# Block sums made in place, residual additions moved forward, and a second small buffer for the attention's features

## The chip, the cores and the metric

The kernel runs on one core of a Trainium2 chip. The metric is the device time of one execution in microseconds. The core has a matrix engine (TensorE, PE in the rows; PEld is its weight load), VectorE (DVE), ScalarE (ACT), GpSimd (POOL) and SyncE (SP), which here only issues DMA transfers. Each engine works through its own queue in order; a wait at the head of a queue holds everything behind it.

## The reference

Two transformer blocks in float32 over 1024 tokens of width 1024. The change touches the end of the first block (windowed attention, its residual and norm) and all of the second:

```python
def rmsnorm(x, g):
    xf = x.astype(jnp.float32)
    y = xf * lax.rsqrt(jnp.mean(xf * xf, axis=-1, keepdims=True) + EPS)
    return (y * g.astype(jnp.float32)).astype(x.dtype)

def short_conv_mixer(h, w_in, conv_w, w_out, on_grid):
    gate_b, gate_c, hv = jnp.split(h @ w_in, 3, axis=-1)
    u = gate_c * hv
    conv = conv3_grid(u, conv_w) if on_grid else conv3_seq(u, conv_w)
    return (gate_b * conv) @ w_out

def swiglu(h, w_in, w_out):
    gate, up = jnp.split(h @ w_in, 2, axis=-1)
    return (jax.nn.silu(gate) * up) @ w_out

# second block
x = x + g1 * short_conv_mixer(modulate(rmsnorm(x, norm1_g[i]), sh1, sc1), ...)
x = x + g2 * swiglu(modulate(rmsnorm(x, norm2_g[i]), sh2, sc2), ...)
return rmsnorm(x, final_g)
```

## The kernel before

Every float32 product is made of three matmuls of a rounded high part and a remainder: a cast on ScalarE (L106) and a subtraction on VectorE (L107) split an operand. The large products of the second block use a scheme of seven block products P1 to P7 in place of eight. It needs sums of blocks: of the activations B11, B12, B21, B22 the sums T1 to T4, of the weights the sums S1 to S4.

The stages, by the trace: mixer A of the first block to some 1010 us; projections and attention to 1620; then in the second block N1, the normed activations' sums and the first weight products (`right_operands`, `eight`, to 1712); the conv mixer's sets (`run_sets`, to 1882), which end with `spill`: a finished group of blocks goes to DRAM and GpSimd makes T1 to T4 from it; the conv mixer's output (`out_products` with `conv_use`, to 1980), where products come in the order P1, P2, P6, P7, P5, P4, P3, each with a use of its four tiles of 128 tokens; N3, the second norm and the first FFN products (to 2067, `third`, `right_operands`, `eight`); the FFN's sets (`run_sets` with `gated_up`, to 2476); its output (`out_products` with `ffn_use`, to 2708).

What sets the order: the program is written in plain order, and the tile scheduler sets each engine's queue by a timeline of its own. Work that runs beside the products is cut into steps, which `mix.tick()` hands out. Buffers come from rings, and a buffer's next writer waits for its last reader. Four things of that kind matter here.

- RAW: a ring of four buffers of 1024 columns (`next_raw`), through which weights to be split, normed tiles (xn), features (hs) and reloaded halves (h1) pass, one after another in the order of the calls.
- Units: 18 pieces of SBUF of 512 columns, `U(i)`, E in the rows. `run_sets` and `spill` take them from a list and put them back; the list is first in, first out. In the FFN's sets a gate's activation (L1706) writes to such a unit, and so do the copies out of PSUM (L1283, L1302).
- pages and raws: in `out_products` an operand comes by DMA into a raw buffer, and its split goes to a page. The conv mixer's output has eight pages and four raws.
- xsr: two buffers of a whole tile, into which `conv_use` and `ffn_use` load the residual x in P4 and P3.

In the attention's tail `keep_half` transposes half a tile (L941), evacuates it into the one buffer of `hs2` on ScalarE (L946) and VectorE (L948) and stores it; `last` squares a tile into `junk`, only to have the sum.

Of the kernel before, what the change touches and what calls it, by code (L numbers as in the profile page):

```python
# [10 lines left out]
ALU = mybir.AluOpType  # L11
# [5 lines left out]
NFF = 22  # L17
# [10 lines left out]
def program(tc, I, out):  # L28
# [4 lines left out]
    with ctx:  # L33
# [145 lines left out]
        mix = Mix()  # L179
# [626 lines left out]
        hs2 = ring([ZX[:, 1024:1536]])  # L806
# [7 lines left out]
        junk = sb(P2, "junk", 512)  # L814
# [357 lines left out]
        def right_operands(where, t, h1, h2, eng):  # L1172
# [104 lines left out]
        def run_sets(sets, where, units):  # L1277
# [12 lines left out]
            for n, (st, use) in enumerate(sets):  # L1290
# [72 lines left out]
        def spill(dst, j, even, odd, units):  # L1363

            (b11, b12), (b21, b22) = even, odd
            ids = [units.get() for _ in range(4)]
            t1, t2, t3, t4 = (U(i) for i in ids)
            if b11 is None:
                ids += [units.get() for _ in range(2)]
                b11, b21 = (U(i) for i in ids[4:])  # L1370
                SY.dma_start(b11, dst["B11"][j])
                SY.dma_start(b21, dst["B21"][j])
            else:
                SY.dma_start(dst["B11"][j], b11)
                SY.dma_start(dst["B21"][j], b21)
# [3 lines left out]
            G.tensor_tensor(t2, b12, t1, ALU.subtract)  # L1379
            SY.dma_start(dst["T2"][j], t2)  # L1380
            G.tensor_tensor(t3, b12, b22, ALU.subtract)
            SY.dma_start(dst["T3"][j], t3)
            G.tensor_tensor(t4, b11, t2, ALU.subtract)
            SY.dma_start(dst["T4"][j], t4)
            units.put(*ids)

        def sums_steps(w, j, dst, a, b):

            def block(m, k):
                return w[(2 * j + k - 1) * 128:(2 * j + k) * 128, (m - 1) * 512:m * 512]  # L1390

            def s0():
                SY.dma_start(a, block(2, 2))
                SY.dma_start(b, block(2, 1))

            def s1():
                G.tensor_tensor(a, a, b, ALU.add)
# [414 lines left out]
```

## Time and profile before

| | |
|---|---|
| median of three runs | 2709.69 us (2708.47 to 2711.11) |
| the profiled execution | 2709.77 us, its span 2708.0 us |
| mean granted clock of TensorE | 0.981 |
| PE busy | 2588.4 us (96%), 13666 matmuls |
| DVE busy | 1841.7 us (68%) |
| ACT busy | 1102.5 us (41%) |
| POOL busy | 656.7 us (24%) |

The span is the time from the first to the last instruction of one execution; 1.8 us lie around it. Busy is the time in which an engine had an instruction in work. PE is idle for 119.6 us; the granted clock is the share of full speed that the chip allowed the matrix engine. What an idle stretch ended with is inferred from the semaphores: the engine and line named are the last that came.

### The profile page before, as it was taken

What the parts mean: (1) busy time and instruction counts of PE and PEld (TensorE: products, weight loads), DVE (VectorE), ACT (ScalarE), POOL (GpSimd) and SP (SyncE); (2) the same over time, 40 slices, a digit from 0 to 9 for tenths busy, and PEclk for the clock granted to TensorE, in tenths of its full rate; (3) what the DMA queues carried; (4) which work ended last, traced back from release to release, by engine and by line L of the source; (5) the groups of instructions that cost most, each with busy time, mean ns of one, the idle gap of its engine ahead of it and who ended that gap; (6) DMA issues with size and microseconds to landing.
All of it is one profiled execution on the core that took longest, in us unless ns stands there. A gap on an engine that the chain in (4) does not pass through costs nothing. (4 is left out here: it accounts for less than half of the span.)

```text
span 2708.0 us, 37147 instructions
## 1 busy us (share of the span) xinstructions
PE 2588.4 (96%) x13666; PEld 2216.0 (82%) x13666; DVE 1841.7 (68%) x3013; ACT 1102.5 (41%) x1979; POOL 656.7 (24%) x634
## 2 busy tenths in 40 slices
PE   8999999999999999999999987999878999999998
PEld 5799998879999778888888876877756877787876
DVE  5677775666778875456677977678566765667536
ACT  4332334322233435345556875223454232334433
POOL 2110000010002412313345762041321345302111
PEclk9999999999999999999999998999989999999999
DMA  7454333364444435541364325356554478538643
GB/s 258 141 148 122 101 119 125 121 205 135 130 137 133 146 103 189 174 155 61 92 244 133 98 78 167 109 183 194 179 181 149 151 253 260 181 103 287 195 151 129
DMA packets 344938, 421.18 MB, mean 156 GB/s; under 512 B 18918, under 2 KB 207870, under 8 KB 344242
## 3 DMA queue, kind: packets, MB, share of 16 engines
q1 hardware_dynamic: 337012, 407.80, 47.0%
q10 hardware_dynamic: 7744, 11.01, 1.1%
q8 instruction: 107, 1.75, 0.3%
q14 instruction: 75, 0.61, 0.1%
HBM read 324.84 MB, written 93.91 MB: 155 GB/s over the span
## 5 line engine op out<-in xcount | busy, mean ns | idle before, releaser
L106 ACT CAST w<-raw 128x1024 fp32r<-128x1024 f32 (+1 forms) x234 | 221.7, 958 | 437.5 <-DMA raw<-in_a_w_in 121.9
L107 DVE TENSOR_TENSOR w<-raw,w 128x1024 fp32r<-128x1024 f32 (+1 forms) x232 | 288.1, 1253 | 152.7 <-ACT w L106 148.3
L1265 PE MATMUL PS<-H,w 128*128 128x512 f32 x1404 | 336.8, 395 | 14.1 <-ACT E L1302 10.7
L1265 PEld LDWEIGHTS PS<-H,w 128*128 128x128 f32 x1404 | 267.2, 191 | 74.5 <-ACT E L1302 12.3
L516 PE MATMUL PS<-H,w 128*128 128x320 f32 x2112 | 320.5, 309 | 1.0 <-DVE TT L525 1.0
L516 PEld LDWEIGHTS PS<-H,w 128*128 128x128 f32 x2112 | 310.8, 188 | 3.1 <-DVE TT L525 1.3
L1456 PE MATMUL PS<-H 128*128 128x512 f32 x924 | 220.4, 397 | 12.3 <-ACT H L106 10.5
L1456 PEld LDWEIGHTS PS<-H 128*128 128x128 f32 x924 | 176.7, 192 | 52.3 <-ACT H L106 12.2
L339 POOL TENSOR_TENSOR H<-ACC,H 128x256 fp32r<-128x256 f32 x52 | 50.3, 968 | 609.6 <-ACT H L338 505.1
L320 DVE SCALAR_TENSOR_TENSOR ACC<-raw,CO,ACC 128x512 f32<-128x512 f32 x182 | 133.8, 747 | 20.6 <-DMA raw<-in_ada_w 17.9
L516 PE MATMUL PS<-H 128*128 128x320 f32 x960 | 144.7, 309 | 0.0
L516 PEld LDWEIGHTS PS<-H 128*128 128x128 f32 x960 | 141.1, 188 | 0.5
L603 PE MATMUL PS<-w,H 128*128 128x512 f32 x600 | 140.1, 391 | 0.0
L1265 PE MATMUL PS<-HB,w 128*128 128x512 f32 x540 | 135.7, 400 | 2.9 <-ACT E L1302 2.5
L603 PEld LDWEIGHTS PS<-w,H 128*128 128x128 f32 x600 | 111.5, 188 | 23.3
L107 DVE TENSOR_TENSOR PTR<-PS,PTR 128x512 fp32r<-128x512 f32 x176 | 106.1, 613 | 35.9 <-ACT PTR L106 34.4
L1265 PEld LDWEIGHTS PS<-HB,w 128*128 128x128 f32 x540 | 102.3, 190 | 28.2 <-ACT E L1302 3.4
L1339 PE MATMUL PS<-H,w 128*128 128x512 f32 x408 | 106.2, 413 | 19.3 <-ACT E L1347 9.1
L392 PE MATMUL PS<-H 128*128 128x512 f32 x510 | 120.9, 391 | 0.0
L870 ACT ACTIVATE s<-s,sm 128x641 f32<-128x641 f32 (+1 forms) x128 | 103.3, 808 | 42.6 <-DVE sm L868 42.0
L107 DVE TENSOR_TENSOR H<-raw,H 128x1024 fp32r<-128x1024 f32 x68 | 88.6, 1306 | 46.6 <-ACT H L106 45.2
L106 ACT CAST H<-raw 128x1024 fp32r<-128x1024 f32 x68 | 70.6, 1043 | 110.1 <-DMA raw<-in_a_w_in 63.2
(356 smaller groups left out, 5201.8 us busy)
## 6 DMA issues: line engine op xcount, KB each, us to landing
raw<-in_a_w_in SPq DMA_DIRECT2D x96, 512.0 KB
raw<-in_ada_w SPq DMA_DIRECT2D x80, 512.0 KB
raw<-in_ffn_w_in SPq DMA_DIRECT2D x76, 256.0 KB
E<-in_ffn_w_out SPq DMA_DIRECT2D x66, 256.0 KB
raw<-in_a_w_out SPq DMA_DIRECT2D x32, 512.0 KB
TFT<-E SPq DMA_DIRECT2D x44, 256.0 KB
SFS<-E SPq DMA_DIRECT2D x44, 256.0 KB
raw<-in_b_w_in SPq DMA_DIRECT2D x20, 512.0 KB
```

The costliest lines, as they stand in the source:

```text
L106: A.copy(hi, src)
L107: turn["split"] = (eng or V).tensor_tensor(lo, src, hif, ALU.subtract)
L320: V.scalar_tensor_tensor(ACC[:, s, :], r[:, j, :], CO[:, c, k:k + 1], ACC[:, s, :], ALU.mult, ALU.add)
L339: G.tensor_tensor(AL.r[:, 256:512], ACC[:, s, c], AL.f[:, 0:256], ALU.subtract)
L392: T.matmul(ps, HT[0][:, k, ap, t * 128:(t + 1) * 128], w[:, k % 2, :], start=k == 0 and n == 0, stop=k == 7 and n == 2)
L516: T.matmul(pss[h][:, 0:320], w[:, k, :], HT[0][:, k, ap, h * 320:(h + 1) * 320], start=k == 0 and n == 0, stop=k == 7 and n == 2)
L603: turn["mm"] = T.matmul(accs[t], ys[j].r[:, ap * 640 + t * 128:ap * 640 + (t + 1) * 128], wv[:, j, :], start=kp == 0 and j == 0 and n == 0 ...
L870: A.activation(out=p[:, :nk + 1], in_=p[:, :nk + 1], func=AF.Exp, scale=-1.0, bias=sm[:, j:j + 1], accum_out=sm[:, 2 + j:3 + j])
L1265: turn["mm"] = T.matmul(ps, w[:, k, :], b[:, ap, k, :], start=start and k == 0 and n == 0, stop=k == 3 and n == 2, skip_group_check=not start)
L1339: turn["mm"] = T.matmul(ps, x[:, k, :], b[:, ap, k, :], start=start and k == 0 and n == 0, stop=stop and k == 3 and n == 2, skip_group_che ...
L1456: turn["mm"] = T.matmul(ps[:, t], x[ap][:, i, t * 128:(t + 1) * 128], s[v][:, i, :], start=new and j + i == 0 and q == 0, stop=j + i == nj ...
```

## The change

- `keep_half`: the ring `hs2` has two buffers; the second is `junk`, into which `last` writes its squares.
- `right_operands`: all four subtractions on VectorE; two were on GpSimd for three of four tiles, in N1 and in N3.
- `spill`: T1 overwrites B21, T3 B22, T2 B12, T4 B11, in that order. It takes no units, but T1, T2 and T4 may only be written when the stores of B21, B12 and B11 have landed. `late_spill` is the form with reloaded B11 and B21.
- `sums`: the steps of two pairs are joined, and the ticks over which they are spread doubled; `run_sets` has one `mix.tick()` more.
- The two outputs share `out_use`. x comes by halves: the first half of tiles 0 to 3 is added in P2 and the second half of tiles 4 to 7 in P5 (`gated_add`: GpSimd multiplies and adds, ScalarE squares; x comes through RAW, and the squares go into the same buffer); the other halves come into units, loaded in P7 and P4. xsr is gone. Normed tiles are made by halves, and a conv tile in P3 takes a RAW buffer more (`tmp`).
- The conv mixer's output has seven pages and six raws.

```diff
@@ attention @@
-        hs2 = ring([ZX[:, 1024:1536]])
+        junk = sb(P2, "junk", 512)
+        hs2 = ring([ZX[:, 1024:1536], junk])
@@ right_operands @@
-            eng.tensor_tensor(b22, b12, b22, ALU.subtract)
+            V.tensor_tensor(b22, b12, b22, ALU.subtract)
             V.tensor_tensor(b12, b12, b21, ALU.subtract)
-            eng.tensor_tensor(b11, b11, b12, ALU.subtract)
+            V.tensor_tensor(b11, b11, b12, ALU.subtract)
@@ run_sets @@
                     head(nxt)
+                mix.tick()
@@ spill @@
-        def spill(dst, j, even, odd, units):
+        def spill(dst, j, even, odd):
             (b11, b12), (b21, b22) = even, odd
-            ids = [units.get() for _ in range(4)]
-            t1, t2, t3, t4 = (U(i) for i in ids)
...
-            G.tensor_tensor(t1, b22, b21, ALU.subtract)
-            SY.dma_start(dst["T1"][j], t1)
...
-            units.put(*ids)
+            for name, x in (("B11", b11), ("B21", b21), ("B12", b12)):
+                SY.dma_start(dst[name][j], x)
+            pair_sums(dst, j, b11, b12, b21, b22)
+        def pair_sums(dst, j, b11, b12, b21, b22):
+            for name, o, x, y in (("T1", b21, b22, b21), ("T3", b22, b12, b22), ("T2", b12, b12, b21),
+                                  ("T4", b11, b11, b12)):
+                G.tensor_tensor(o, x, y, ALU.subtract)
+                SY.dma_start(dst[name][j], o)
@@ sums, in the conv's and the FFN's sets @@
-                    mix.begin(sums(c_out, 4, SC, [units.get() for _ in range(4)]), 5)
+                    mix.begin(sums(c_out, 4, SC, [units.get() for _ in range(4)]), 12)
...
-                    mix.begin(sums(f_out, NFF // 2, SF, [units.get() for _ in range(4)]), NFF - 9)
+                    mix.begin(sums(f_out, NFF // 2, SF, [units.get() for _ in range(4)]), 2 * (NFF - 9))
@@ the outputs @@
+        def out_use(X, name, t, ps, done):
+            u2, u3, r, x = U(t), U(4 + t), U(8 + t), U(12 + t)
+            def gated_add(u, gb, i, h):
+                G.tensor_tensor(u, u, gb, ALU.mult)
+                y = next_raw()[:, 0:512]
+                SY.dma_start(y, X[i][:, h * 512:(h + 1) * 512])
+                G.tensor_tensor(u, u, y, ALU.add)
+                mean_square(MS[:, i, h:h + 1], u, y)
+            if name in ("P1", "P6"):
+                A.copy(u2, ps)
+            elif name == "P2":
+                V.tensor_tensor(r, ps, u2, ALU.add)
+                gated_add(r, gbs[0], t, 0)
+            elif name == "P7":
+                SY.dma_start(x, X[t][:, 512:1024])
+            elif name == "P5":
+                A.copy(u3, ps)
+                V.tensor_tensor(u3, PS[:, 4 + t], u3, ALU.add)
+                gated_add(u3, gbs[1], 4 + t, 1)
+            elif name == "P4":
+                V.tensor_tensor(u2, ps, u2, ALU.add)
+                V.tensor_tensor(u2, u2, gbs[1], ALU.mult)
+                V.tensor_tensor(u2, u2, x, ALU.add)
+                SY.dma_start(x, X[4 + t][:, 0:512])
+                mean_square(MS[:, t, 1:2], u2, PS[:, 4 + t])
+                done(t, r, u2)
+            else:
+                tmp = next_raw()[:, 0:512]
+                V.tensor_tensor(tmp, ps, gbs[0], ALU.mult)
+                V.tensor_tensor(x, x, tmp, ALU.add)
+                mean_square(MS[:, 4 + t, 0:1], x, tmp)
+                done(4 + t, x, u3)
...
-        out_products(c_out, 4, TC, SC, pages[2:], [p.f[:, q * 1024:(q + 1) * 1024] for p in pages[:2] for q in range(2)],
+        out_products(c_out, 4, TC, SC, pages[3:], [p.f[:, q * 1024:(q + 1) * 1024] for p in pages[:3] for q in range(2)],
```

Line numbers shift by a few: L1302 keeps its number, the gate's L1706 becomes L1705, the transposes' L1484 L1479, N1's and N3's products L1339 L1340, the output's matmuls L1456 L1451; the multiplication and the addition of `gated_add` are L1608 and L1611.

ScalarE in the FFN's sets, before, from the last copy of one set to the first casts of the next, around the first gate after a `spill`. In brackets stands what a row waits for: DMAHW is a DMA, Pool GpSimd.

```order
L1302 COPY E_13956<-PS_176 128x512 [waits PE_49]
L1706 ACTIVATE E_13956<-E_13956 128x512 [waits DMAHW1_49,DVE_49,Pool_49]
L1302 COPY E_13956<-PS_176 128x512 [waits DMAHW0_49,PE_49]
L106 CAST w2_179<-raw2_183 128x512 [waits DMAHW2_49,PE_49]
L1706 ACTIVATE E_13956<-PS_176 128x512 [waits PE_49]
L106 CAST PA_13953<-raw2_183 128x512 [waits PE_49]
L106 CAST w3_180<-raw3_13954 128x1024 [waits DMAHW7_49,DVE_49,Activation_49]
```

The same place after:

```order
L1302 COPY E_13956<-PS_176 128x512 [waits PE_49]
L1283 COPY E_13956<-PS_176 128x512 [waits PE_49]
L1705 ACTIVATE E_13956<-E_13956 128x512 [waits DVE_49]
L106 CAST w3_180<-raw1_182 128x512 [waits DMAHW5_49,PE_49]
L1705 ACTIVATE E_13956<-PS_176 128x512 [waits PE_49]
L106 CAST PA_13953<-raw1_182 128x512 [waits DMAHW3_49,PE_49]
L1302 COPY E_13956<-PS_176 128x512 [waits DMAHW4_49,PE_49,Pool_49]
L106 CAST w0_177<-raw0_181 128x1024 [waits DMAHW2_49,DVE_49,Activation_49]
```

The gate's activation on a unit (L1706, now L1705) no longer waits for a DMA and GpSimd, and the DMA and GpSimd wait has gone to a later copy, L1302.

GpSimd at P5 in the conv mixer's output, before (L1638 and L1642 are the multiplications of P2 and P5, L1652 the additions of P4, L927 a power for the norm):

```order
L1652 TENSOR_TENSOR E_13956<-E_13956 128x512
L1638 TENSOR_TENSOR E_13956<-E_13956 128x512
L1642 TENSOR_TENSOR E_13956<-E_13956 128x512 x4
L927 TENSOR_TENSOR RM_13958<-RM_13958,mhalf_188 128x1 x2
L1652 TENSOR_TENSOR E_13956<-E_13956 128x512 x2
L927 TENSOR_TENSOR RM_13958<-RM_13958,mhalf_188 128x1 x2
```

And after:

```order
L1608 TENSOR_TENSOR E_13956<-E_13956 128x512 x2
L1611 TENSOR_TENSOR E_13956<-E_13956,raw3_13954 128x512
L1608 TENSOR_TENSOR E_13956<-E_13956 128x512
L1611 TENSOR_TENSOR E_13956<-E_13956,raw1_182 128x512
L1608 TENSOR_TENSOR E_13956<-E_13956 128x512
L1611 TENSOR_TENSOR E_13956<-E_13956,raw0_181 128x512
L1611 TENSOR_TENSOR E_13956<-E_13956,raw1_182 128x512
L927 TENSOR_TENSOR RM_13958<-RM_13958,mhalf_188 128x1 x8
```

The additions of P5 now stand between its multiplications, each on a RAW buffer. On SyncE the buffer raw3 then takes a load of `ffn_w_in`, and after that the last load of `conv_w_out` for P4, with the loads of x for tiles 6 and 7 between; before, the loads of `conv_w_out` stood ahead of P5.

## Rows read from the trace of the kernel before

**Rows 1.** What PE waits for, whole span: engine, releaser, us in total, times, longest.

```profile
PE PS L1484 <- ACT raw L1489: 13.2, 6, 4.1
PE PS L1265 <- ACT E L1302: 13.2, 6, 4.9
...
PE PS L1339 <- ACT w L106: 7.7, 4, 4.5
...
PE PS L998 <- ACT ZX L946: 4.1, 3, 2.3
...
PE PS L1265 <- ACT E L1283: 2.0, 1, 2.0
```

**Rows 2.** Timeline of PE in the FFN's sets: start, us, work, [idle before <- releaser].

```profile
2215.72 7.36 PE L1265 MATMUL PS<-H,w 128*128 128x512 f32 x24 [2.41 <-ACT E L1302]
...
2247.78 2.96 PE L1265 MATMUL PS<-HB,w 128*128 128x512 f32 x12
...
2259.26 7.38 PE L1265 MATMUL PS<-H,w 128*128 128x512 f32 x24 [2.99 <-ACT E L1302]
...
2306.09 6.20 PE L1265 MATMUL PS<-H,w 128*128 128x512 f32 x14 [4.93 <-ACT E L1302]
```

**Rows 3.** Timeline of ScalarE at the same places.

```profile
2214.56 0.63 ACT L1706 ACTIVATE E<-E 128x512 f32<-128x512 f32 x1 [13.69 <-DMA TFT<-E]
...
2258.10 0.63 ACT L1706 ACTIVATE E<-E 128x512 f32<-128x512 f32 x1 [14.74 <-DMA TFT<-E]
...
2304.93 0.63 ACT L1706 ACTIVATE E<-E 128x512 f32<-128x512 f32 x1 [16.21 <-DMA TFT<-E]
```

**Rows 4.** Timeline of SyncE's DMA issues: B21 and T4 of one pair.

```profile
2200.74 0.37 SPq L1375 DMA_DIRECT2D TFB<-E  x1
...
2209.92 0.38 SPq L1384 DMA_DIRECT2D TFT<-E  x1
```

**Rows 5.** Stretches: busy us of PE, PEld, DVE, ACT, POOL; clock, DMA share, GB/s.

```profile
1920.00:1925.00 5.00, 4.71 (x11) 3.79 (x12) 4.71 (x3) 2.32 (x3) 4.86 (x3) 0.50 0.63 204
...
1995.00:2000.00 5.00, 1.17 (x5) 0.77 (x5) 4.07 (x11) 3.47 (x8) 0.55 (x1) 0.50 0.82 271
...
2305.00:2310.00 5.00, 3.91 (x9) 3.14 (x10) 4.07 (x6) 2.56 (x5) 2.31 (x2) 0.52 0.56 197
```

**Rows 6.** Timeline in the conv's P6: PE, SyncE, ScalarE.

```profile
1920.29 11.93 PE L1456 MATMUL PS<-H 128*128 128x512 f32 x39 [6.32 <-ACT H L106]
...
1909.10 7.38 SPq L121 DMA_DIRECT2D H<-SCS  x2
...
1919.19 1.04 ACT L106 CAST H<-H 128x1024 fp32r<-128x1024 f32 x1 [2.94 <-DMA H<-SCS]
```

**Rows 7.** Groups in 1950 to 2030: shapes, count | busy us, mean ns | idle before.

```profile
L922 ACT ACTIVATE E<-E 128x512 f32<-128x512 f32 x16 | 10.1, 629 | 17.8 <-DVE E L1655 8.0 <-DVE E L1664 7.5 <-DVE RM L926 1.3
...
L1652 POOL TENSOR_TENSOR E<-E 128x512 f32<-128x512 f32 x2 | 2.6, 1291 | 4.0 <-DMA E<-X 4.0
...
L107 DVE TENSOR_TENSOR w<-raw,w 128x1024 fp32r<-128x1024 f32 x1 | 1.2, 1226 | 3.8 <-ACT w L106 3.8
```

**Rows 8.** Timeline, P5 to N3: ScalarE, GpSimd, VectorE, PE.

```profile
1952.35 0.58 ACT L1640 COPY E<-PS 128x512 f32<-128x512 f32 x1
...
1954.57 7.02 POOL L1642 TENSOR_TENSOR E<-E 128x512 f32<-128x512 f32 x4 [29.71 <-DVE E L1641]
...
1963.07 0.69 DVE L1653 TENSOR_TENSOR E<-PS,E 128x512 f32<-128x512 f32 x1 [2.63 <-PE PS L1456]
...
1999.95 3.35 PE L1339 MATMUL PS<-H,w 128*128 128x512 f32 x7 [0.54 <-ACT H L1167]
```

**Rows 9.** Timeline of VectorE and GpSimd side by side.

```profile
2442.60 1.67 DVE L1245 TENSOR_TENSOR raw<-raw 128x512 f32<-128x512 f32 x1
...
2442.04 1.68 POOL L1377 TENSOR_TENSOR E<-E 128x512 f32<-128x512 f32 x1 [1.23 <-DVE E L1708]
```

**Rows 10.** Timeline of ScalarE in N1.

```profile
1663.35 1.14 ACT L1167 CAST HB<-E 128x512 fp32r<-128x512 f32 x2 [2.69 <-POOL E L1179]
```

More of the change, by code (lines that the diff above doesn't have):

```diff
@@ L1421, in sums @@
             steps = []
             for j in range(0, nj, 2):
-                two = [sums_steps(w, i, dst, U(bufs[2 * (i - j)]), U(bufs[2 * (i - j) + 1])) for i in range(j, min(j + 2, nj))]
-                for x in zip(*two) if len(two) == 2 else [(y,) for y in two[0]]:
-                    steps.extend(x)
+                two = [pair(j + i, U(bufs[2 * i]), U(bufs[2 * i + 1])) for i in range(min(2, nj - j))]
+                steps.extend(lambda x=x: [y() for y in x] for x in zip(*two))
             return steps
@@ L1549, in program @@
             halves[n]["late"](N1, (2 * n, 2 * n + 1), late_uses[n])
-        units = Units(14, 15, 8, 9, 10, 11, 12, 13)
-        spill(TC, 0, (None, U(16)), (None, U(17)), units)
-        units.put(16, 17)
+        late_spill(TC, 0, U(16), U(17), U(14), U(15))
+        units = Units(8, 9, 10, 11, 12, 13, 14, 15, 16, 17)
         c_sets = []
@@ L1578, in use @@
                 free()
-                spill(TC, j, *((cv[:, 0:512], cv[:, 512:1024]) for cv in cvs), units)
+                spill(TC, j, *((cv[:, 0:512], cv[:, 512:1024]) for cv in cvs))
                 cvs.clear()
                 if j == 1:
-                    mix.begin(sums(c_out, 4, SC, [units.get() for _ in range(4)]), 5)
+                    mix.begin(sums(c_out, 4, SC, [units.get() for _ in range(4)]), 12)
                 mix.tick()
@@ L1672, in program @@
+            if name == "P3" and t < 3:
+                if t:
+                    halves[t + 1]["load"]()
+                halves[t + 1]["early"](N3, ((0, 6), (1, 7), (2, 0))[t], early_up(t + 1))
         pages = slot_pages((4, 2, 3, 5, 1))
-        out_products(c_out, 4, TC, SC, pages[2:], [p.f[:, q * 1024:(q + 1) * 1024] for p in pages[:2] for q in range(2)],
+        out_products(c_out, 4, TC, SC, pages[3:], [p.f[:, q * 1024:(q + 1) * 1024] for p in pages[:3] for q in range(2)],
                      conv_use)
@@ L1695, in program @@
             if f % 2:
-                spill(TF, f // 2, (None, U(ys[0])), (None, U(ys[1])), units)
-                units.put(*ys)
+                b11, b21 = units.get(), units.get()
+                late_spill(TF, f // 2, U(ys[0]), U(ys[1]), U(b11), U(b21))
+                units.put(*ys, b11, b21)
                 ys.clear()
@@ L1711, in use @@
                 if f % 2:
-                    spill(TF, f // 2, *((U(a), U(b)) for a, b in ys), units)
+                    spill(TF, f // 2, *((U(a), U(b)) for a, b in ys))
                     units.put(*ys[0], *ys[1])
@@ L1729, in program, with fourth @@
             SY.dma_start(gbs[m], GT[4][m, :].partition_broadcast(128))
-        xsr = ring([U(12, 2), U(14, 2)])
-        def fourth(i, halves):
+        def fourth(i, *xs):
             rms(RX[:, i:i + 1], MS[:, i, :])
```

151 lines of the change are left out of this document (41 added, 110 removed).

## The prediction, as recorded before the run

> **What bounds the kernel now.** TensorE. The reader starts with the busy times: PE works 2588.4 of the span's 2708.0 us, so 119.6 us are idle and an edit can win only from those, from the low clock that follows a stop, or lose by adding to them. The second view is the table of PE's waits [rows 1]: the largest groups lie in the parts that the change rewrites. The third is the timeline around the stops.
>
> In the FFN's sets PE stops at 2215.72, 2259.26 and 2306.09, each time for a copy of ScalarE (L1302) [rows 2]. ScalarE has the gate's activation L1706 queued ahead of it, and that one waits 13.7, 14.7 and 16.2 us for a store of T sums [rows 3]: its output goes to a unit that `spill` took for T4, and T4's store, issued at 2209.92, lets ScalarE go only at 2214.56, 13.8 us after the pair's B21 went out at 2200.74 [rows 3, 4]. In the conv mixer's output PE stops 6.3 us at 1920.29: SyncE held two loads for 7.4 us because the four raw buffers were not free, and the cast came 2.9 us after the last of them [rows 6]. At the change from conv to FFN the transposes wait 13.2 us in all for the evacuations [rows 1].
>
> After a stop the granted clock is low: 0.52 in the 5 us around the end of the stop of 4.9 us, 0.50 after that of 6.3 us [rows 5]; 0.50 is the lower of its two levels, 1.2 GHz. So a stop is paid twice. Twelve matmuls take 2.96 us, 0.24 each; the 24 after the first two stops took 7.36 and 7.38 instead of 5.8, the 14 after the third 6.20 instead of 3.4 [rows 2].
>
> **The change part by part.** Times are against the profiled run, 2709.77 us (span and 1.8 around it), 0.1 us above the median.
>
> *In-place T sums.* `spill` takes no units any more, T1 to T4 overwrite the pair. In the new order the gate's activation after a pair waits for VectorE alone (the order of ScalarE above); the next writer of a unit that a T store still reads comes 146 matmuls or more, some 35 us, after the pair is complete, where before it came after some 14. T1 now waits for B21's store, which adds a landing of 2 to 5 us to a chain of four subtractions and their stores that took 13.8 us; 35 minus 19 leaves 16 us. So three stops go: 2.41 + 2.99 + 4.93 = 10.3 us, and with them 1.6 + 1.6 + 2.8 = 6.0 us of slow matmuls. The loads of the next weights stand behind T1 and T3 on SyncE, but stood behind T1, T2 and a sum before. The least is nothing, if a weight load becomes late instead; the most 16. I take -15. In the conv's sets one stop of 2.0 us, for a copy into a unit (L1283 [rows 1]), goes for the same reason: -2 (0 to -2.5).
>
> *Six raws and seven pages.* The two loads that were held 7.4 us find buffers; the stop of 6.3 us goes and so do 3 us at half clock (4.7 us of matmuls at 0.50 [rows 5] and a remainder). Four T's of the last pair come one store later, before their first reader still. -8.5 (-5 to -9.5).
>
> *Right operands on VectorE.* Six subtractions in N1 go to VectorE, some 0.69 us each like L1653 [rows 8], 4 us in all. ScalarE's weight casts, for which PE waited 7.7 us in all there and in N3, 4.5 at once [rows 1], stood at 1664.40 right behind casts that waited 2.7 us for a subtraction of GpSimd [rows 10]; now they stand ahead of them. Of the wait and some 1.2 us at a low clock behind it I count most, less what VectorE's longer queue takes back: -4 (-6 to 0).
>
> *Attention.* The second buffer for hs takes away the wait for the store of the features between a tile's halves; the thrown-away squares now wait for that store instead, and later products start a little later. PE's waits for the features' evacuation, 4.1 us [rows 1], are the most that can go, and I count 3 of them lost again: -1 (-4 to +3).
>
> *Additions moved into P2, P5 and P7.* This part costs. In P5, tile t's second half is multiplied and added on GpSimd, squared on ScalarE, and the x it adds sits in a RAW buffer. The RAW ring has four buffers, and the load of `ffn_w_in` behind it and the two loads of `conv_w_out` for P4 take the same buffers in turn. Count from T0, the end of P5's tile 0, which the first L1640 copy dates at 1952.35 [rows 8]. GpSimd's first multiplication begins 2.2 us later [rows 8], its order is mult, mult, add, mult, add, mult, add, add, each 1.29 us alone [rows 7] or 1.76 as the four L1642 took [rows 8]. The third ends at 6.1 to 7.5; the square (0.63 [rows 7], and some 0.2 to read its sum) frees raw3 at 7 to 8.3; a load with its issue takes some 2.9 (the distance in [rows 6]); cast 1.04 [rows 6] and subtraction 1.23 [rows 7] free raw3 again at 12 to 13.5; the second load lands at 15 to 16.5. The cast that feeds P4 also stands behind the square of tile 3, whose x could be loaded only after tile 1's square: 2.2 + 5 operations + 0.8 + 2.9 + one more addition + 0.8 is 14.5 to 17.3. With the cast P4 starts at 16 to 18.5. PE has 24 matmuls until then, 5.8 us: a new stop of 10 to 13 us, where none is now, with 2.4 us of half clock behind it. I take a start at 17.5, near the upper end, because VectorE does two-input work there. Before, P4's tile 0 was done at T0 + 10.7 (L1653 at 1963.07 [rows 8]); after, 17.5 + 30 matmuls of 0.24 + 2.4 = 27. From there to the first N3 product it took 36.9 us before (1999.95 [rows 8]) with x loads late between; after, the rest of P4 and P3 (60 matmuls, 14.3 us) and then eight groups of transposes in a row, whose evacuations, splits and additions on VectorE I put at 15 to 20 us: 29 to 34, say 32. Sum: 27 + 32 against 47.6, so +11. The best is -2 (no stop), the worst +16.
>
> *N3's second half.* Six RAW takes a tile instead of five, but no late x: +1 (-2 to +5). *FFN output*: the same additions lie behind long products, the P5 to P4 turn used the ring that way already: 0 (-2 to +2). `fourth` is the same work.
>
> Sum: -15 - 2 - 8.5 - 4 - 1 + 11 + 1 = -18.5. **2709.8 - 18.5 = 2691 us.**
>
> One row on the sharing of two engines: beside GpSimd's subtraction of 1.68 us at 2442.04 VectorE's L1245, with two inputs in SBUF, took 1.67 us [rows 9], where an instruction of that size without such company takes 0.69 [rows 8]. The Trainium skill, "SBUF — State Buffer", section "Who interferes with whom", says that a VectorE instruction with two SBUF inputs and a GpSimd instruction that reads SBUF lock each other out for a whole instruction, whichever began first. By that rule GpSimd's eight operations in P5 lie near 1.76 and the total is 2692; by uncontended 1.29 throughout it is 2689. The row agrees with the rule.
>
> **The rivals.**
> *The RAW ring's stop does not come.* The loads could be ordered kindly by chance, or GpSimd could start earlier. For: the row order is only an order. Against: each link is a buffer reuse. Then +11 is -2: 2678.
> *The FFN's stops stay.* ScalarE no longer waits for T4, but the T stores landed late because so much was in flight; the weight casts that stand right behind L1302 could be the next to wait. Against: PE's stops there now all end at L1302. Then -15 is 0: 2706, no change.
> *Slower: N3 stays at the lower clock.* Before, PE ran at 0.50 in 1995 to 2000 [rows 5], among the waiting transposes, until N3's products ran dense. After, tile by tile, a chain through tmp, xn, hs and h1 could be longer than a tile's products; four tiles of 48 matmuls and their transposes are some 14 us each, 56 in all (an estimate from 0.24 a matmul), and at half clock over half of them the loss is 28 us: 2719. It decides if a tile's chain takes over some 18 us. Against: I add up 13.6 us for it, the tile's additions, square, evacuations and splits at the prices of [rows 7, 8].
> *The change doesn't do what it says* for units: the list of units could hand a T unit back at once, and the FFN's and the conv's stops would stay: -17 is 0, 2708. The order above speaks against it.
>
> **How the numbers follow.** The forecast has 0.62, its own range is 2683 to 2699. No ring stop 0.15, FFN stops stay, for either reason, 0.14, low clock in N3 0.06, something unnamed 0.03. The range 2677 to 2707 takes the first three in. A measurement tells some 0.2%, 5.4 us, from no change. Faster: 0.62 + 0.15 + 0.04 of the third = 0.81. Same: 0.11. Slower: 0.08.
>
> **What would show it.** In the trace after: no wait of ScalarE's gate for a T store in the FFN's sets, and PE's waits for L1302 down from 13.2 to about 3; no 6.3 us stop in the conv's P6; a stop of some 10 to 13 us right before P4's first matmul, ended by the cast of a `conv_w_out` load; about 59 us from P5's tile 0 to N3's first product. Wrong would be: the FFN part of the span not shorter by over 10 us, or the stretch of the conv's end not longer.

## The result and the profile after

The changed kernel takes 2735.4 us (median of four runs, 2733.3 to 2736.1) against 2710.4 us of the kernel before beside it: a ratio of 1.0092, 95% interval 1.0074 to 1.0109. It is 25 us slower, where 2691 us was forecast with 2707 us as the upper end. The profiled execution took 2735.2 us, its span 2733.4 us, at a mean granted clock of 0.977 (0.981 before).

What PE waits for in the changed kernel, whole span (engine, releaser, us in total, times, longest), beside [rows 1]:

```profile
PE PS L1451 <- ACT H L106: 20.9, 5, 11.0
PE PS L1265 <- ACT E L1302: 11.7, 4, 5.1
...
PE PS L1479 <- ACT raw L1484: 9.2, 3, 4.0
PE PS L941 <- DVE ZX L934: 7.2, 3, 5.6
PE PS L1340 <- ACT w L106: 6.5, 4, 2.5
...
PE PS L1479 <- DVE raw L1647: 3.1, 2, 2.2
```

Three things are to be seen. The waits for L1302, 13.2 us before, are still 11.7: most of the gain that carried the forecast did not come. The output's matmuls (L1451) now wait 20.9 us for casts (10.5 before), 11.0 at once. And one wait has grown, in the attention's transposes (L941, 2.6 us before), and one is new, in N3's (L1479 behind L1647).

Where the 25.4 us of span came in is read by pairing the same matmul in both traces: the table gives its start in a kernel's trace less that in the trace of before. Of the experiments, which come below, the columns stand here too. "End" is the difference of the spans. The end of the FFN's sets is taken at 2500, where matmuls are paired by their number in PE's order (13666 in each trace): at 2476 no one matmul stands for it, because the changed kernel makes sixteen matmuls of the output ahead of the sets' last twelve where the kernel before makes three. In code that no kernel changed (up to 1500) the traces differ by -3.1 to +2.0 us, so a step of the table is good to 2 us or so. A row is one execution each, and not the median one: those of e4, e7 and e10 were 4.4 to 4.7 us below the medians given with the experiments, that of e13 3.6 us above.

```text
time before      1500  1623  1714  1844  1937  1973  2016  2078  2500  2640   end
after            +1.0 +10.0  +4.6  +2.3  +1.9 +21.5 +18.4 +34.9 +30.9 +30.8 +25.4
e1_hs            -2.1  -0.8  -5.7  -8.0  -8.6 +10.8  +7.5 +23.7 +24.0 +24.0 +18.6
e2_sums          -3.1  +5.9  +0.5  -1.9  -2.2 +15.1 +11.5 +27.4 +24.3 +24.5 +19.1
e3_right          0.0  +8.8  +9.5  +7.2  +7.1 +24.7 +21.2 +36.1 +30.3 +30.2 +24.8
e4_conv          +0.9 +10.0  +5.0  +2.7  +2.4  +2.6  +4.5  +7.6  +0.6  +0.5  -4.9
e5_raws          -1.1  +7.0  +2.1  -0.3  -2.6  +3.9  +5.1 +21.0 +19.9 +20.1 +14.8
e6_tmp           -1.0  +8.1  +2.9  +0.5   0.0 +17.2 +13.7 +16.6  +9.6  +9.7  +4.3
e7_defer         -0.6  +7.7  +2.7  +0.3  -1.5  +1.0  -1.8  +1.1  -2.1 -10.7 -16.5
e10_spill        -1.0  +8.0  +2.3  +2.1  -3.9 +12.9  +9.6 +26.0 +25.3 +25.2 +19.8
e11_nosum        +2.0 +10.7  +5.5  +3.2  +1.1 +19.9 +16.1 +32.1 +11.8 +11.7  +6.5
e12_defer_hs     -0.6  +0.7  -4.2  -6.6 -10.5  -4.4  -5.2  -3.3  -8.6 -17.2 -23.0
e13_e7raws       +1.2 +10.2  +4.5  +2.2  +1.5  +1.9  +0.7  +4.3  +1.6  -7.0 -12.8
e15_five         -2.1  -2.0  -7.1  -9.4 -12.3 -11.9 -12.9 -12.0 -15.3 -23.8 -29.6
```

Read along the first row: the attention's tail loses 9.0 (1500 to 1623), N1 wins 5.4 back, the conv's sets 2.3; from 1937 to 2016, P5 to the first products of N3, 16.5 are lost, in N3 another 16.5; the FFN's sets win 4.0, their output up to 2640 nothing, and the end 5.4: from the last matmul to the end it takes 8.1 us (2725.4 to 2733.4) where it took 13.4 (2694.6 to 2708.0).

The places on PE's timeline (start, us, work, [idle before <- releaser]): the attention's tail, P4, N3, and three stops of the FFN's sets.

```profile
1624.87 1.97 PE L941 MATMUL PS<-ident,ZX 128*128 128x128 f32 x8 [5.57 <-DVE ZX L934]
...
1976.01 10.27 PE L1451 MATMUL PS<-H 128*128 128x512 f32 x32 [11.04 <-ACT H L106]
...
2063.67 1.10 PE L1479 MATMUL PS<-ident,raw 128*128 128x128 f32 x4 [2.19 <-DVE raw L1647]
2066.41 5.16 PE L1340 MATMUL PS<-H,w 128*128 128x512 f32 x12 [1.65 <-ACT w L106]
...
2320.92 3.06 PE L1265 MATMUL PS<-HB,w 128*128 128x512 f32 x12 [2.40 <-ACT E L1302]
...
2342.89 4.92 PE L1265 MATMUL PS<-HB,w 128*128 128x512 f32 x12 [5.10 <-ACT E L1302]
...
2387.55 4.60 PE L1265 MATMUL PS<-HB,w 128*128 128x512 f32 x12 [3.44 <-ACT E L1302]
```

The twelve matmuls of N3 at 2066.41 took 5.16 us where twelve take 2.96 [rows 2]: the stretch 2065 to 2070 has a clock of 0.50, the lower of the two levels.

```profile
2065.00:2070.00 5.00, 3.54 (x8) 2.34 (x9) 2.45 (x4) 2.48 (x4) 0.00 (x0) 0.50 0.01 5
```

### The profile page after: what moved, and what is told of

The parts are those of the page before. It is cut to its first block, busy times and chain, and to the rows that moved or that the text cites. A ratio compares the mean times of both kernels' runs of the same rounds, so it can differ in the third digit from the quotient of the medians.

```text
span 2733.4 us, 37183 instructions
## 1 busy us (share of the span) xinstructions
PE 2598.9 (95%) x13666; PEld 2221.6 (81%) x13666; DVE 1834.6 (67%) x3033; ACT 1104.8 (40%) x1979; POOL 637.2 (23%) x622
## 3 DMA queue, kind: packets, MB, share of 16 engines
q8 instruction: 107, 1.75, 0.3%
## 4 chain that ended last, share of the span: by engine, by line
PE 73%; DMA 9%; DVE 7%; POOL 4%; issue 3%; ACT 3%; SPq 1%; POOLq 0%; DVEq 0%; ACTq 0%
PE PS L516 15%; PE PS L1265 12%; PE PS L1451 8%; PE PS L603 7%; PE PS L676 5%; PE PS L392 5%; PE PS L1340 5%; PE PS L1053 3%; PE PS L998 3%; PE PS L861 2%; DMA E<-in_ffn_w_out 2%; PE PS L883 2%; PE PS L895 2%; DMA raw<-in_ffn_w_in 2%; PE PS L497 1%
## 5 line engine op out<-in xcount | busy, mean ns | idle before, releaser
L107 DVE TENSOR_TENSOR w<-raw,w 128x1024 fp32r<-128x1024 f32 (+1 forms) x232 | 296.4, 1287 | 191.3 <-ACT w L106 189.4
L1265 PEld LDWEIGHTS PS<-H,w 128*128 128x128 f32 x1404 | 267.1, 190 | 61.8 <-ACT w L106 3.9
L1451 PE MATMUL PS<-H 128*128 128x512 f32 x852 | 206.3, 401 | 26.7 <-ACT H L106 20.9
L1451 PEld LDWEIGHTS PS<-H 128*128 128x128 f32 x852 | 164.8, 194 | 65.3 <-ACT H L106 23.3
L1374 POOL TENSOR_TENSOR E<-E 128x512 f32<-128x512 f32 x60 | 101.1, 1685 | 364.3 <-DMA TFB<-E 104.7
L1265 PE MATMUL PS<-HB,w 128*128 128x512 f32 x540 | 137.7, 404 | 11.9 <-ACT E L1302 11.7
L516 PEld LDWEIGHTS PS<-H 128*128 128x128 f32 x960 | 141.1, 188 | 0.5
L1392 POOL TENSOR_TENSOR E<-E 128x512 f32<-128x512 f32 x60 | 93.0, 1556 | 148.7 <-DMA E<-in_ffn_w_out 90.9
L107 DVE TENSOR_TENSOR H<-raw,H 128x1024 fp32r<-128x1024 f32 (+1 forms) x69 | 91.8, 1334 | 52.4 <-ACT H L106 49.6
L1340 PE MATMUL PS<-H,w 128*128 128x512 f32 x408 | 106.7, 414 | 19.5 <-ACT E L1348 8.6
```

The source lines that it names most:

```text
L107: turn["split"] = (eng or V).tensor_tensor(lo, src, hif, ALU.subtract)
L516: T.matmul(pss[h][:, 0:320], w[:, k, :], HT[0][:, k, ap, h * 320:(h + 1) * 320], start=k == 0 and n == 0, stop=k == 7 and n == 2)
L1265: turn["mm"] = T.matmul(ps, w[:, k, :], b[:, ap, k, :], start=start and k == 0 and n == 0, stop=k == 3 and n == 2, skip_group_check=not start)
L1340: turn["mm"] = T.matmul(ps, x[:, k, :], b[:, ap, k, :], start=start and k == 0 and n == 0, stop=stop and k == 3 and n == 2, skip_group_che ...
L1374: G.tensor_tensor(o, x, y, ALU.subtract)
L1451: turn["mm"] = T.matmul(ps[:, t], x[ap][:, i, t * 128:(t + 1) * 128], s[v][:, i, :], start=new and j + i == 0 and q == 0, stop=j + i == nj ...
```

## Experiments

Each kernel's time stands against runs of the kernel before on the same chip. e1 to e6, e10 and e11 change one part of the changed kernel; e7 builds on e6, and e12, e13 and e15 build on e7.

### The attention: the features' one buffer again

```diff
-        junk = sb(P2, "junk", 512)
-        hs2 = ring([ZX[:, 1024:1536], junk])
+        hs2 = ring([ZX[:, 1024:1536]])
...
+        junk = sb(P2, "junk", 512)
```

> The changed kernel with one part undone: the features of the attention's last tiles have their one buffer again, and the thrown-away squares have a buffer of their own. In the changed kernel TensorE stands 5.57 us at 1624.87 on VectorE's L934, behind ScalarE's junk square L1015, and N1's first product starts 13.2 us late; at the first conv set 4.6 us of that are left. Theory (the shared buffer orders a square of normed_x behind work that the tail doesn't need): the 5.57 us stop goes, N1's first product is late by under 6 us, the whole takes 2735 - 5 to 2735 - 10, that is 2725 to 2730 us. Rival (the lateness comes from the right operands on VectorE, which share that stretch): the stop stays within 1 us and the time within 2733 to 2738.

Measured (e1_hs): 2726.53 us, ratio 1.0058 (1.0038 to 1.0078). The attention's tail loses 1.3 us instead of 9.0, the stop is back to the 2.56 us that the kernel before had at this place. PE, before and in e1_hs:

```profile
1614.87 1.24 PE L941 MATMUL PS<-ident,ZX 128*128 128x128 f32 x8 [2.56 <-DVE ZX L934]
```

```profile
1612.91 1.97 PE L941 MATMUL PS<-ident,ZX 128*128 128x128 f32 x8 [2.56 <-DVE ZX L934]
```

What held it in the changed kernel is seen on ScalarE there. L946 writes features, L1015 is a thrown-away square, L922 the square whose sum the next norm needs:

```profile
1613.29 0.45 ACT L946 ACTIVATE junk<-PS,C 128x128 f32<-128x128 f32 x1
...
1620.60 0.72 ACT L1015 ACTIVATE junk<-r,SM 128x512 f32<-128x512 f32 x1 [4.06 <-DVE SM L1013]
...
1621.44 0.72 ACT L1015 ACTIVATE junk<-r,SM 128x512 f32<-128x512 f32 x1
...
1622.29 0.63 ACT L922 ACTIVATE junk<-r 128x512 f32<-128x512 f32 x1
```

Before, L922 wrote into ZX and came ahead of L1015:

```profile
1612.07 0.63 ACT L922 ACTIVATE ZX<-r 128x512 f32<-128x512 f32 x1
...
1613.56 0.72 ACT L1015 ACTIVATE junk<-r,SM 128x512 f32<-128x512 f32 x1 [0.77 <-DVE SM L1013]
```

Features, two kinds of squares and their stores now share `junk`, and its users keep the order of the program. So L922 stands behind two squares of L1015, the first of which waits 4.06 us for VectorE's L1013, and L934 and the transposes follow. The theory holds for the stop and the time. But the stop explains only 3.0 us of the loss (5.57 against 2.56): counted by the number of the matmul, PE was late by 1.0 us at 1500 and by 7.1 already at 1616.33, ahead of the stop, in small stops of up to 1.3 us. e1 takes these away too. Whether they come from sharing `junk` or from the second buffer as such is not shown: no run gives the features a second buffer of their own.

### The column sums' steps as before

```diff
-                mix.tick()
...
-                    mix.begin(sums(f_out, NFF // 2, SF, [units.get() for _ in range(4)]), 2 * (NFF - 9))
+                    mix.begin(sums(f_out, NFF // 2, SF, [units.get() for _ in range(4)]), NFF - 9)
```

The conv's sums likewise (5 ticks), and one pair's step per turn.

> The changed kernel with one part undone: the column sums of the output weights go back to one unit's step per tick (half as many ticks, 5 and 15 sets instead of 12 and 30 ticks). In the changed kernel three stops of TensorE in the FFN sets (2.40, 5.10, 3.44 us) stand on ScalarE's gate L1302, behind ScalarE's cast L106, which waits for weights that SyncE issued behind the stores of the sums. Theory (joint steps put the stores of two sums, and so their waits, ahead of the weight loads): ScalarE's waits of L106 on the weights fall from 34.6 us to under 10, the three stops go, and with the clock that they take the time is 2718 to 2728 us. Rival (the loads are late because of the in-place T sums, whose stores must end before the next y): the waits stay above 25 us, and the time is 2731 to 2738.

Measured (e2_sums): 2729.2 us, 1.0070 (1.0051 to 1.0088), between the two ranges. The three stops are still there (2.78, 4.67, 2.62 us), ScalarE still waits 25.5 us for weights in the FFN's sets, and these win 3.1 us as against 4.0. The theory falls; the 6 us come from elsewhere: 4.1 of them are there at 1500, in code that no kernel changed, and P4's stop is 9.0 instead of 11.0 us.

### No column sums in the FFN's sets

```diff
-                    mix.begin(sums(f_out, NFF // 2, SF, [units.get() for _ in range(4)]), 2 * (NFF - 9))
+                    four = [units.get() for _ in range(4)]
+                    SY.dma_start(U(four[0]), f_out[0:128, 0:512])
+                    def stores(names, j):
+                        return lambda: [SY.dma_start(SF[n][j + i], U(four[0])) for n in names for i in range(min(2, NFF // 2 - j))]
```

> The changed kernel without the column sums of the FFN's output weights: GpSimd's sums and the loads of their operands are left out, SyncE still stores 44 tiles of the same size to the same places, from one loaded tile, so the FFN's output is computed with other weights in four of its seven products. Theory (SyncE holds the weight loads of the FFN sets behind stores that wait for GpSimd's sums, which wait for their loads): ScalarE's waits of L106 on the weights fall from 31 us in six waits to under 10, the three stops of TensorE (2.40, 5.10, 3.44 us) go, and the time is 2720 to 2728 us. Rival (the weights are late because of the stores of the in-place T sums): the waits stay above 20 us and two or three stops of over 2 us stay, time 2730 to 2737.

Measured (e11_nosum): 2716.0 us, 1.0026 (1.0015 to 1.0037), 4 us below the theory's range. The FFN's sets win 20.3 us, no stop over 0.9 us is left in them, and no wait on a weight's DMA stands among ScalarE's larger ones there. So it is not the steps' grouping but the sums themselves, their loads and GpSimd's work, that hold the weights back; the two were left out together. How, is seen on SyncE of the changed kernel, which from 2300 to 2345 waits 18.4 us for GpSimd's sums (L1392),

```profile
SPq L1393 <- POOL E L1392: 18.4, 11, 3.6
```

and in particular ahead of the stop at 2342.89. L1401 and L1405 load a sum's operand, L1393 stores a sum, L1375 a T sum, L1218 loads weights:

```profile
2332.82 0.38 SPq L1405 DMA_DIRECT2D E<-in_ffn_w_out  x1
2335.05 0.32 SPq L1393 DMA_DIRECT2D SFS<-E  x1
2335.42 1.28 SPq L1405 DMA_DIRECT2D E<-in_ffn_w_out  x1
2337.28 0.32 SPq L1375 DMA_DIRECT2D TFT<-E  x1
2337.66 1.04 SPq L1218 DMA_DIRECT2D raw<-in_ffn_w_in  x2
```

and ScalarE's cast of those weights, behind which L1302 stands:

```profile
2341.73 0.62 ACT L106 CAST w<-raw 128x512 fp32r<-128x512 f32 x1 [7.69 <-DMA raw<-in_ffn_w_in]
```

### The T sums into units of their own

```diff
-            pair_sums(dst, j, b11, b12, b21, b22)
+            ids = [units.get() for _ in range(4)]
+            t1, t2, t3, t4 = (U(i) for i in ids)
+            for name, o, x, y in (("T1", t1, b22, b21), ("T2", t2, b12, t1), ("T3", t3, b12, b22), ("T4", t4, b11, t2)):
+                G.tensor_tensor(o, x, y, ALU.subtract)
+                SY.dma_start(dst[name][j], o)
+            units.put(*ids)
```

> The changed kernel with one part undone: the T sums of the sets go into four units of their own again, in the order T1, T2, T3, T4, and not in place. Theory (the in-place sums are what freed ScalarE's gate from its 55.5 us of waits on the T stores, and this is the gain of the FFN sets): the gate waits on stores again, the FFN sets take 6 to 12 us more than in the changed kernel, the time is 2740 to 2748 us. Rival (that wait was covered, the sets are set by the weights): the sets take the same within 3 us, time 2732 to 2738.

Measured (e10_spill): 2733.97 us, 1.0093 (1.0080 to 1.0106): the time of the rival with the mechanism of the theory. ScalarE's gate (L1710 here) waits for T stores again, engine and releaser, us, times, longest:

```profile
ACT E L1710 <- DMA TFT<-E: 54.3, 4, 17.3
```

and the FFN's sets win 0.7 us instead of 4.0: in place is worth 3.3 us there, less than the theory's 6. In the conv's sets the stop of before is back too (1.84 us at 1795.63; before 1.95, in the changed kernel none). But from 1844 to 2016 this kernel loses 7.5 us instead of 16.1. Some 6 of these 8.6 us come between 1908 and 1924 of the time before, where PE's stop ahead of P6 is gone. In the changed kernel PE, ScalarE and GpSimd show there:

```profile
1923.32 12.81 PE L1451 MATMUL PS<-H 128*128 128x512 f32 x48 [4.13 <-DVE E L1617]
...
1920.36 1.04 ACT L106 CAST H<-H 128x1024 fp32r<-128x1024 f32 x1 [6.22 <-DMA H<-TCT]
...
1908.18 7.17 POOL L1374 TENSOR_TENSOR E<-E 128x512 f32<-128x512 f32 x4 [56.53 <-DMA TCB<-E]
```

GpSimd may make the last pair's sums only when the stores of the blocks have landed, at 1908.18, and the last sum goes out at 1915.37; before it went out at 1903.47, here at 1908.12. ScalarE waits 6.22 us to cast a loaded T sum, behind that cast stand its copies of P1 (L1615), and VectorE's evacuation of P2 (L1617), which releases PE, needs these. Here, with six raws as well, PE goes into P6 without a stop (one of 1.93 us stands ahead of P2's second half):

```profile
1918.23 2.90 PE L1456 MATMUL PS<-H 128*128 128x512 f32 x12
```

P4's stop is shorter too (7.66 us), and the stop of 4.4 us that the changed kernel has at P1 is not there. For that one the cause is open: P1's operand is cast at 1884.56 here and at 1887.62 there, and PE comes some 4 us later here, after a stop of 2.18 us at 1855.94. The three loads of P7's x (L1620) that the changed kernel's SyncE issues ahead of these operands take it 0.4 us each; a load of P2's x (L1610 at 1877.29) waits 2.4 us for its raw buffer. In sum, in place won in the sets what it cost in the conv's output: the ratios are 1.0092 with it and 1.0093 without.

### The right operands

```diff
-            right_operands(N1, t, a, b)
+            right_operands(N1, t, a, b, G if t < 3 else V)
```

with two of the subtractions on `eng`, in N3 likewise.

> The changed kernel with one part undone: two of the right operands' four subtractions for the first three tiles of N1 and of N3 go back from VectorE to GpSimd. In the changed kernel N1 (1623 to 1712 of the time before) gains 5.4 us, the 4.5 us stop at 1666.44 being gone; the kernel with the features' one buffer gained the same 4.9 us there. Theory (that gain is the right operands' move to VectorE): the stop comes back, N1 gains under 1.5 us, and the time is 2738 to 2742 us. Rival (the gain comes from the sums on GpSimd or the order around them): N1 keeps its 4 to 6 us and the time is within 2732 to 2738.

Measured (e3_right): 2738.21 us, 1.0114 (1.0097 to 1.0131), in the theory's range, though the interval overlaps that of the changed kernel. N1 loses 0.7 us where the changed kernel wins 5.4, and its stop is back:

```profile
1675.16 5.06 PE L1340 MATMUL PS<-H,w 128*128 128x512 f32 x11 [4.50 <-ACT w L106]
```

### The conv's output: the old use

```diff
-            out_use(X2, name, t, ps, third)
+            u2, u3, r = conv_out_use(name, t, ps)
...
+            elif name == "P4":
+                xs = xsr()
+                SY.dma_start(xs, X2[t])
...
+                third(t, xs, r)
```

> The changed kernel with one part undone: the conv's output products use their results as before (two-tile buffers xs, residual x not through the raw ring, squares of a whole tile's halves at the end), while the six raw buffers stay and the FFN's output keeps the new code. In the changed kernel TensorE idles 27.5 us from 1937 to 2014 against 14.1 before, with one stop of 11.04 us at 1976.01, and N3 loses 17 us more (15.7 against 8.2 us idle, the rest at a granted clock of .50 to .87). Theory (the ring of raws, given to the residual loads and squares too, is what stops P4, and the lower clock in N3 comes from late operands behind it): the 11 us stop goes, N3's products run at a clock above .95, and the time is 2700 to 2712 us. Rival (N3 is slower because its right operands are all on VectorE): the stop goes but N3 still takes 10 us or more longer than before: 2717 to 2726.

Measured (e4_conv): 2709.61 us, 0.9996 (0.9985 to 1.0007). P5 to N3's products loses 2.1 us instead of 16.5, N3 3.1 instead of 16.5, and the FFN's sets win 7.0. N3's clock is not above .95 throughout as the theory has it: three stretches of 5 us have 0.70 to 0.84. The new use of the results in the conv's output holds nearly all of the loss; right operands on VectorE don't slow N3.

### Four raws and five pages

```diff
-        out_products(c_out, 4, TC, SC, pages[3:], [p.f[:, q * 1024:(q + 1) * 1024] for p in pages[:3] for q in range(2)],
+        out_products(c_out, 4, TC, SC, pages[2:], [p.f[:, q * 1024:(q + 1) * 1024] for p in pages[:2] for q in range(2)],
```

(`pages` counts slots of two pages.)

> The changed kernel with one part undone: the conv's output products have four raw buffers and five pages again, instead of six and four. Theory (the ring is the bound between P5 and P4): with two buffers fewer the stop at P4, 11.04 us, grows to 15 to 30 us and P6's stop of 6.3 us may come back; the time is 2740 to 2760 us. Rival (the stop is set by SyncE's queue of residual loads and not by the number of buffers): the stop stays within 2 us of 11, and the time within 2731 to 2739.

Measured (e5_raws): 2724.24 us, 1.0054 (1.0035 to 1.0073), outside both: between P5 and P4 PE stands 3.6 us in two stops instead of 14.9 in three, and P6's stop is 3.9 us against 4.1. Fewer raw buffers are better here, not worse. That the fifth slot of pages lets P4's first operands be split while P5 runs fits the trace (their weights went out at 1943.6, not 1951.7), but was not separated from the rest.

### P3's product out of the raw ring

```diff
-                tmp = next_raw()[:, 0:512]
-                V.tensor_tensor(tmp, ps, gbs[0], ALU.mult)
-                V.tensor_tensor(x, x, tmp, ALU.add)
-                mean_square(MS[:, 4 + t, 0:1], x, tmp)
+                V.tensor_tensor(u2, ps, gbs[0], ALU.mult)
+                V.tensor_tensor(x, x, u2, ALU.add)
+                mean_square(MS[:, 4 + t, 0:1], x, u2)
```

> The changed kernel with one buffer moved: the product of the last gate in P3's use goes into the tile's unit U(t), as before the change, and no longer into a buffer of the raw ring. In the changed kernel VectorE does this step (L1634) for P3's four tiles at 2008, 2011, 2057 and 2082, before the change at 1970, 1973, 1979 and 1980; N3's products run from 2032 on. Theory (P3's evacuations stand in the raw ring behind N3's weight loads, so the last two tiles' features come in the middle of N3, and its stops take the clock): the four steps come within 15 us of each other, N3 loses under 5 us instead of 15, the 11 us stop at P4 stays, and the time is 2717 to 2724 us. Rival (N3 is slow because of the stop at P4 ahead of it): N3's loss stays at 12 to 17 us, time 2731 to 2737.

Measured (e6_tmp): 2717.09 us, 1.0035 (1.0021 to 1.0048). The step on VectorE, in the changed kernel:

```profile
2008.16 0.68 DVE L1634 TENSOR_TENSOR raw<-PS,E 128x512 f32<-128x512 f32 x1
...
2011.11 0.68 DVE L1634 TENSOR_TENSOR raw<-PS,E 128x512 f32<-128x512 f32 x1
...
2057.30 0.69 DVE L1634 TENSOR_TENSOR raw<-PS,E 128x512 f32<-128x512 f32 x1
...
2081.71 0.68 DVE L1634 TENSOR_TENSOR raw<-PS,E 128x512 f32<-128x512 f32 x1
```

and in this one:

```profile
1992.14 0.68 DVE L1633 TENSOR_TENSOR E<-PS,E 128x512 f32<-128x512 f32 x1
1992.80 0.68 DVE L1633 TENSOR_TENSOR E<-PS,E 128x512 f32<-128x512 f32 x1
...
2001.63 0.69 DVE L1633 TENSOR_TENSOR E<-PS,E 128x512 f32<-128x512 f32 x1
2002.56 0.68 DVE L1633 TENSOR_TENSOR E<-PS,E 128x512 f32<-128x512 f32 x1
```

N3 loses 2.9 us instead of 16.5; P4's stop stays (9.1 us). In the changed kernel a tile's `tmp` had its turn in the ring behind the N3 weights of the tile before it. By the order of the takes in the program, the two weights between make it, for the last two tiles, the buffer that held the features of the tile before, and in the trace its step follows directly on a split of that tile's operands (L1169 at 2056.58, the step at 2057.30). So the last two tiles came one behind the other, 24.4 us apart, they could be normed only in the middle of N3, and their transposes stopped PE there. e6 itself takes the buffer out of the ring altogether; that its place counts and not only its number is read from the trace.

### P5's residuals behind P4's weights

On top of that:

```diff
                 V.tensor_tensor(u3, PS[:, 4 + t], u3, ALU.add)
-                gated_add(u3, gbs[1], 4 + t, 1)
             elif name == "P4":
+                gated_add(u3, gbs[1], 4 + t, 1)
```

> As the kernel with the P3 product in U(t), and in addition P5's residual loads (four buffers of the raw ring) stand behind P4's two weight loads in the program, in P4's use. In the changed kernel these two loads were issued at 1951.7 and 1971.2, against 1878.2 and 1882.6 before it. Theory (the loads of P4's weights wait for their turn in the ring behind the residuals): they are issued over 20 us earlier, the stop of 11 us at P4 goes, and with the P3 product moved the time is 2704 to 2713 us. Rival (the stop is SyncE's queue or the pages): the stop stays above 7 us and the time within 2715 to 2724.

Measured (e7_defer): 2697.96 us, 0.9961 (0.9949 to 0.9973). SyncE's issues of P4's two weight loads, in the changed kernel

```profile
1951.69 0.37 SPq L121 DMA_DIRECT2D raw<-in_conv_w_out  x1
...
1971.15 0.38 SPq L121 DMA_DIRECT2D raw<-in_conv_w_out  x1
```

and in this one

```profile
1938.20 0.42 SPq L121 DMA_DIRECT2D raw<-in_conv_w_out  x1
...
1940.90 0.37 SPq L121 DMA_DIRECT2D raw<-in_conv_w_out  x1
```

Only the second was moved by over 20 us, but the stop is gone: PE goes from P5 into all 48 matmuls of P4,

```profile
1949.60 5.76 PE L1451 MATMUL PS<-H,HB 128*128 128x512 f32 x24
1955.20 11.08 PE L1451 MATMUL PS<-H 128*128 128x512 f32 x48
```

The move changes the loads' place both in the ring and on SyncE's queue. In the changed kernel's trace the ring fits link by link: ScalarE's square frees a buffer at 1964.74 and a load of `ffn_w_in` goes out at 1964.76; VectorE's split of it ends at 1971.13 and P4's second load goes out at 1971.15. SyncE stood at a store (L1646) until 1964.00, waiting 11.9 us for GpSimd's first addition, which the ring waited for too.

The kernel is faster than expected because `out_use` serves the FFN's output too: there three stops at P4 (2.4, 1.7 and 1.3 us in the kernel before, at 2628 to 2640) go as well, with their slow clock 8.6 us between 2550 (-2.1) and 2640 (-10.7). The changed kernel had them too (2.37, 1.69 and 0.80 us), and no step of the prediction looked there for a gain.

### Both losses taken out, and the raws once more

> The kernel with the P3 product in U(t) and P5's residual loads behind P4's weight loads (2697.96 us), and in addition the features' one buffer and the own buffer of thrown-away squares in the attention. Theory (the two losses are apart in time and add): the attention's 8 us come off, 2688 to 2692 us, 0.7% under the kernel before. Rival (the later start was absorbed by a wait further on): 2694 to 2699.

Measured (e12_defer_hs): 2686.08 us, 0.9919 (0.9905 to 0.9933), 2 us below the theory's range: the features' one buffer adds to the two moves.

> The kernel with the P3 product in U(t) and P5's residual loads behind P4's weight loads, with four raw buffers and five pages for the conv's output products instead of six and four. Theory of the prediction (six raws remove the stop of 6.3 us ahead of P6 and its clock, 8.5 us): 2704 to 2709 us. Rival (the stop ahead of P6 is there with either, 4.0 us with six and 3.9 with four beside the ring's traffic): within 3 us of 2698.

Measured (e13_e7raws): 2693.43 us, 0.9946 (0.9931 to 0.9962), below both ranges. Six raws did not give the 8.5 us: P6's stop is 3.8 us with four and 4.0 with six. But the two stops have different causes. With four ScalarE waits for a load of weights' sums, as in [rows 6],

```profile
1920.84 1.04 ACT L106 CAST H<-H 128x1024 fp32r<-128x1024 f32 x1 [4.38 <-DMA H<-SCS]
```

and with six for a load of a T sum, 5.88 us (6.22 in the changed kernel). Of all the kernels only e10, with six raws and T sums in units of their own, has no stop there.

> The best kernel so far (P3 product in U(t), P5's residual loads behind P4's weight loads, the features' one buffer: 2686.08 us) with four raw buffers and five pages for the conv's output products, as before the change. With the features' two buffers the same step went from 2697.96 to 2693.43 us. Theory (six raws cost what a page fewer takes, some 4 us): 2679 to 2684 us. Rival (that difference was the spread of two runs): within 2 us of 2686.

Measured (e15_five): 2681.50 us, 0.9907 (0.9887 to 0.9927), in the range of the theory. The intervals overlap in both pairs, so what four raws win is not settled; the ratios put it at 4.1 us in the one pair and 3.3 in the other. This kernel is the fastest, 0.9% under the kernel before and nearly 2% under the changed one.

## Why the prediction was wrong, by its own steps

The measured steps add up: +1.0 (to 1500) + 9.0 - 5.4 - 2.3 - 0.4 + 16.5 + 16.5 - 4.0 - 0.1 - 5.4 = 25.4 us. Forecast was -18.5. Five steps missed by 50 us in all, and some 6 us were won where less or nothing was forecast; that makes the 44 us between.

- **N3's second half, +1, measured +16.5.** The largest miss. "Six RAW takes a tile instead of five" was counted by number, not by place. `tmp` is taken behind N3's weights of the tile before it. The rival that N3 stays at the lower clock had the outcome (2719, 28 us) and too small a chance; its test, a chain of over some 18 us a tile, was decided the wrong way, because the 13.6 us added up durations only and left out the turn in the ring; 24.4 us lay between the last two tiles. e6 shows what the take costs, 13.6 of the 16.5 us.
- **Attention, -1 (up to +3), measured +9.0.** "The thrown-away squares now wait for that store instead" is not what the trace shows: the one ahead of the stop waits for VectorE's L1013. That the needed square L922 would stand behind them was not looked for. That stop is 3 us of the loss; the other 6 came in small stops ahead of it, whose cause is open. e1 shows that nearly all of it hangs on the second buffer being `junk`, or being there.
- **FFN's sets, -15, measured -4.0.** The gate's waits for T stores did go, but PE still stood 11.7 us in four stops, 10.3 in three before. In place of [rows 3] ScalarE waits for weights, 31.4 us in six waits. This was the rival at 2706, in its own words "the weight casts that stand right behind L1302 could be the next to wait". e11 shows that the weights' sums make them late; e10 puts the worth of in place at 3.3 us.
- **Six raws, -8.5, measured -0.4 with P1's new stop in it.** The stop of 6.3 us [rows 6] became one of 4.1. The loads that were held did go out, but the step "Four T's of the last pair come one store later, before their first reader still" was wrong: ScalarE waited 6.22 us for one of these sums. e10 shows it, with six raws, T sums in units and no stop there. P1 got a stop of 4.4 us, whose cause is open.
- **P5 to P4, +11, measured +16.5 to N3's first products.** The mechanism, counted from buffer to buffer, held: a stop of 11.04 us (10 to 13 said), P4's start 19.8 us after the first L1622 copy at 1956.24 (16 to 18.5 said), N3's first product 61.8 us after it (59 said). The size was short: the two loads on the way took 4.1 and 3.8 us from issue to cast, where 2.9 each was said. e7 shows that the place of P5's loads makes the stop.

Right were the right operands (-4, measured -5.4; e3 takes it away) and the conv's sets (-2, measured -2.3: the stop at L1283 is gone, and back in e10). For the FFN's output 0 (-2 to +2) was said, "the same work". That held up to 2640, but the end won 5.4 us: less is left to do behind the last matmul. This gain of additions moved forward was not looked for. No run undoes it alone, but all kernels with `out_use` there have it, e4 too.

The trace after has both prices for GpSimd's P5 steps: 1.75 us each for the first two multiplications at 1958.27 beside VectorE's additions and splits, 2.25 for the addition at 1961.73 beside a split, and 1.26 each for the three steps from 1965.18, when VectorE was idle. The eight took 12.5 us of work, between the 10.3 and 14.1 of the two prices. The rule of the Trainium skill cited ("SBUF — State Buffer", "Who interferes with whom") has them take longer only beside a VectorE instruction with two inputs in SBUF, such as the splits; the trace agrees. Between the two prices lay 3 us of the sum (2689 and 2692); they explain none of the miss.

## What to carry to other kernels

A ring is a queue: a new user costs by what stands ahead of it in program order, and by who stands behind it, so write down the order of the takes across the stages, not their number. When a wait goes away, follow the queue that fed it and not only the waiting engine: the next wait on that queue may stand right behind it. A result made in place must wait for the store of what it overwrites, so look for its next reader too, and not only for the buffers that become free. A buffer that gets a second purpose also gets a second order to keep.

## What the runs showed of the hardware

Before, N3 ran at a granted clock of 1.00 from 2005 on, with stops of 1.7 us and less between its products, as in the stretch

```profile
2050.00:2055.00 5.00, 3.58 (x14) 2.30 (x14) 5.00 (x7) 3.11 (x7) 1.68 (x1) 1.00 0.35 105
```

After, with stops of 2.5 us at 2052.46 and 2.2 us at 2063.67, 0.81 to 0.87 was granted from 2050 to 2065 and 0.50 in 2065 to 2070. Of N3's 16.5 us some 7.5 are idle time (15.7 us of it against 8.3) and the rest goes with the low clock: late operands cost twice there, as a single stop does.
